# An out projection made of seven block products per half of its inner dimension, with one pooling projection moved ahead

## The chip, the cores and the metric

The kernel runs on one core of a Trainium2 chip. The metric is the device time of one execution in microseconds (us), lower is better; the time before is the median of three runs. One further execution was taken with the hardware profiler. Engines are named as in the profile: PE is TensorE (matmuls), DVE VectorE, ACT ScalarE, POOL GpSimd, SP SyncE; SP and POOL issue most DMAs here.

## The reference

One layer of a streaming encoder on 512 tokens, all in fp32:

```python
h = rmsnorm(x, norm_mix_pre)                 # 512 x 2048
proj = h @ w_in                              # 2048 x 5120: u_pool (1024), q, f, i, g (1024 each)
y_pool = pool_mixer(u_pool, ...)             # windowed means, 4 groups of 256: (mean - u) @ pool_w + b
y_hgrn = hgrn2_mixer(q, f, i, g, ...)        # gated recurrence, 8 heads of 128
mix = concatenate([y_pool, y_hgrn]) @ w_out  # 512 x 2048 @ 2048 x 2048, the "out projection"
x = x + rmsnorm(mix, norm_mix_post)
h = rmsnorm(x, norm_mlp_pre)
ff = square(relu(h @ w_mlp_in)) @ w_mlp_out  # 2048 x 8192 and back
x = x + rmsnorm(ff, norm_mlp_post)
```

## The kernel before

**Precision.** Every matmul operand of the large projections is split in two parts, hi (a cast on ACT) and lo (raw minus hi, a subtraction on DVE), and a product is the sum of three matmuls: hi·hi, hi·lo and lo·hi. A weight block of 512 x 512 (1 MB, "room") is loaded raw by SP, and its split takes two casts and two subtractions of 128 x 1024, by halves.

**Order.** The kernel is written out by hand: each engine takes its instructions in the order in which the Python issues them. Two lists help. `clock` holds generators ("tasks": gates, scores, outputs, pooling), of which each takes a step at a tick, and a tick comes after each block of 12 matmuls. `mplan` and `plan` are tables that say what is issued at which slot of the products. The input projection runs in ten groups of 512 columns, `proj_order`; pooling halves are U0 and U1, the recurrence's halves F, Q, V, G with 0 or 1. `outputs(c)` finishes the recurrence's half c and `task()` of `pool_chunk(c)` the pooling's half c; both also store signed copies into DRAM (`stash`, tile `mix_dram`).

**Out projection.** The left half of the output columns (tiles `om`) is computed plainly: 2 groups x 4 weight blocks x 4 row tiles x 12 = 384 matmuls. The right half uses a form of Strassen's scheme with seven products instead of eight (`ORDER`, numbers 1, 2, 5, 3, 6, 7, 4). The work of one product with one weight block is here called a slot: 24 matmuls of 128 x 512. The right half takes 14 slots, (product, inner half q) in pairs. A slot needs a weight operand and an activation operand. The weight operands of products 1, 5, 6 and 4 live in the same room, which is not reloaded but refilled: after the split of product 1's block a POOL DMA adds another block of `w_out` to it in place, and so on. Products 5, 3, 6 and 7 take activation sums made from `mix_dram` (tiles `sr`), split by `split_sum`. The split for slot m+1 is issued at the start of slot m. Results go from the PSUM banks `oa` and `og` to Y by ACT copies or DVE adds (`evac_half`), and are then squared (ACT) and weighed (DVE).

The MLP that follows uses the same seven products for all of its work and makes up the time from 668 us on.

Of the kernel before, what the change touches and what calls it, by code (L numbers as in the profile page):

```python
# [28 lines left out]
def hybrid_block(  # L29
# [334 lines left out]
    proj_order = (U0, F0, Q0, V0, G0, F1, Q1, V1, G1, U1)  # L364
# [3 lines left out]
    mix_rows = (2, 0, 3, 1)  # L368
    for n in range(2):
        for r in mix_rows:  # L370
            wlist.append((w_out, r, n))
# [82 lines left out]
    mixp = {}  # L454

    def stash(c, q, k, src, scales):

        sg = junk_tile([P, 512], "signed").rearrange("p (t s) -> p t s", t=2)
        for t in range(2):
            nc.scalar.activation(out=sg[:, t], in_=src[:, t * 256:(t + 1) * 256], func=AF.Copy,  # L460
                                 scale=scales[(t + 1 + c) % 2])
        nc.gpsimd.dma_start(mix_dram[c, q].rearrange("t p k s -> p t k s")[:, :, k, :], sg)


    def pool_chunk(c, tags):
# [14 lines left out]
        def task():  # L480
# [21 lines left out]
            dh, dl = new_pair(f"pd{c}")  # L502
# [22 lines left out]
            if c:  # L525
                add(A, B, 4, 7, hi2)
                add(B, A, 8, 15, hi2)
                yield 1
            diff(1, *ws[1])
            split(1, hi2, ws[1][1])  # L530
            yield 1
            ph, pl = new_pair(f"mp{c}")
            mixp[("p", c)] = (ph, pl)
            for g, (w, s) in enumerate(ws):
                for o in range(2):
                    ps = pss.tile([P, 512], F32, tag="s", name="pps")
                    for ct in range(2):
                        wh, wl = (pw[:, k, g, ct, o * P:(o + 1) * P] for k in range(2))
                        j = 2 * g + ct
                        nc.tensor.matmul(ps, wh, dh[:, j], start=ct == 0, stop=False)  # L540
                        nc.tensor.matmul(ps, wh, dl[:, j], start=False, stop=False)
                        nc.tensor.matmul(ps, wl, dh[:, j], start=False, stop=ct == 1)
                    j = 2 * g + o
                    y = U[:, j, PAD:]
                    nc.vector.tensor_scalar(out=y, in0=ps, scalar1=vcol("pb", 4 * c + j),
                                            scalar2=vcol("pscale", 4 * c + j), op0=ALU.add, op1=ALU.mult)
                    nc.scalar.copy(out=ph[:, j, :], in_=y)
                    nc.vector.tensor_tensor(out=pl[:, j, :], in0=y, in1=ph[:, j, :].bitcast(F32), op=ALU.subtract)
                    stash(c, 1, j, y, (1.0, -1.0))
                    yield 1  # L550
# [4 lines left out]
    class Hgrn:  # L555
# [156 lines left out]
        def outputs(self):  # L712
# [20 lines left out]
            ph, pl = new_pair(f"mh{c}")  # L733
            mixp[("h", c)] = (ph, pl)
# [5 lines left out]
            for h in range(4):  # L740
                ps = pss.tile([P, 512], F32, tag="s", name="ops")
                for w in range(NT):
# [3 lines left out]
                nc.scalar.activation(out=ph[:, h, :], in_=ps, func=AF.Copy, scale=g)  # L746
                nc.vector.scalar_tensor_tensor(out=pl[:, h, :], in0=ps, scalar=g, in1=ph[:, h, :].bitcast(F32),
                                               op0=ALU.mult, op1=ALU.subtract)
# [17 lines left out]
    clock.add(lower_bound_task(), 14)  # L766
    for ci, c in enumerate(proj_order):
        gemm_group(f"pj{c}", xT, c not in (V0, V1, G0, G1), evacs[c],
                   feeder=feed_x if ci == 0 else None)
        if c == U0:  # L770
            clock.add(pt0(), 1)
        elif c == U1:
            clock.add(pt1(), 1)
        elif c in (F0, F1):
            clock.add(hgr[c == F1].gates(), 1)
        elif c in (G0, G1):
            clock.add(hgr[c == G1].outputs(), 1)


    class MixActs:  # L780
        order = (("h", 0), ("p", 0), ("h", 1), ("p", 1))

        def __len__(self):
            return 4

        def __getitem__(self, i):
            return mixp[self.order[i]]

    ss_m = const.tile([P, NT, 4], F32, name="ss_m")
    X, YZ, HI, LO, A = {}, {}, {}, {}, {}  # L790

    def late_pools():
# [30 lines left out]
    ss2 = const.tile([P, NT], F32, name="ss2")  # L823
# [37 lines left out]
    def keep_x2(t):  # L861
        Y = late["Y"]
        n_out = (D, D, D // 2, 0)[t]
        if n_out < D:
            nc.sync.dma_start(x2_dram[t * P:(t + 1) * P, 0:D - n_out], Y[t][:, 0:D - n_out])
        if n_out:
            nc.sync.dma_start(out2d[t * P:(t + 1) * P, D - n_out:D], Y[t][:, D - n_out:D])

    def norm2_task():
        for t in range(NT):  # L870
            yv = late["Y"][t]
            nc.scalar.activation(out=yv, in_=yv, func=AF.Square, accum_out=ss2[:, t:t + 1])
# [7 lines left out]

    def evac_mix(n):
        def f(t, bank):
            if n == 0 and t == 0:
                late_pools()
            yv = late["Y"][t][:, n * 512:(n + 1) * 512]
            junk = junk_tile([P, 512], "junk")
            nc.scalar.activation(out=junk, in_=bank, func=AF.Square, accum_out=ss_m[:, t, n:n + 1])
            nc.vector.tensor_tensor(out=yv, in0=bank, in1=late["wpost"][n // 2][:, n % 2 * 512:n % 2 * 512 + 512],
                                    op=ALU.mult)
        return f  # L890

# [100 lines left out]
    def feed_in(tp, u, engine):  # L992

        dst = raw_in(tp, 1 + u // 2, u % 2)
        for k2 in range(2):
            ps = pss.tile([P, 2, 256], F32, tag="s", name="fps")
            for k in range(2):
                c = u * 512 + (2 * k2 + k) * P
                for t in range(2):
                    nc.tensor.transpose(out=ps[:, k, t * P:(t + 1) * P],  # L1000
                                        in_=late["Y"][2 * tp - 2 + t][:, c:c + P], identity=ident)
# [9 lines left out]
    S, SR = {}, {}  # L1011

    def new_sum(i):
        S[i] = pairs.tile([P, 2, 8, 256], F32R, tag="pp", name=f"s{i}")

    def split_sum(i, q):
        src = SR[i][:, 4 * q:4 * q + 4]
        a = S[i][:, :, 4 * q:4 * q + 4]
        if i == 7:
# [7 lines left out]
    def split_sum_step(i, q):  # L1027
        return lambda: split_sum(i, q)

    def load_sums():  # L1030
        yield 1
        for nm, (i0, i1) in (("53", (5, 3)), ("67", (6, 7))):
            room = pairs.tile([P, 2, 8, 256], F32, tag="pp", name=f"sr{nm}")
            SR[i0], SR[i1] = room[:, 0], room[:, 1]
        for q in range(2):
            qs = slice(4 * q, 4 * q + 4)
            for i, (c, tp) in ((7, (0, 1)), (5, (1, 1)), (6, (0, 0)), (3, (1, 0))):
                nc.sync.dma_start(SR[i][:, qs], mix_dram[c, q, tp])
            yield 1

    def sums_task(q):

        a5, a7, a6, a3 = (SR[i][:, 4 * q:4 * q + 4] for i in (5, 7, 6, 3))
        for dst, src in ((a5, a7), (a7, a6), (a6, a5), (a3, a6)):
            nc.vector.tensor_tensor(out=dst, in0=dst, in1=src, op=ALU.add)
            yield 1

    mslots = [(i, q) for i in ORDER for q in range(2)]

    def mix_block(a, b, q):  # L1050
        return w_out[mix_rows[2 * a - 2 + q], 1 + b]

    def mix_split_gen(m):
        if m >= len(mslots):
            yield from split_gen(m - len(mslots))
# [12 lines left out]
        if more:  # L1068
            load_mix(raw, *more, q, True)
        elif i == 2:  # L1070
            load_mix(raw, 2, 2, q)
        elif i == 4:
            load_x(q)
        elif q == 0:
            load_yz(0)

    MY = {}

    def load_mix(raw, a, b, q, add=False):
        src = mix_block(a, b, q)  # L1080
# [22 lines left out]
    for n in range(2):  # L1103
        if n == 1:
            clock.add(load_sums(), 2)
            MY[0] = YZ[0]
            MY[1] = [late["tp2"].tile([P, 2, 512], F32, tag="tmp", bufs=4, name=f"my{h}") for h in range(2)]
            clock.add(sums_task(0), 9)
# [613 lines left out]
```

## Time and profile before

| what | value |
|---|---|
| median of three runs | 1925.89 us (1925.26 to 1927.15) |
| the profiled execution | 1927.38 us, its span 1925.7 us |
| input projection and recurrence | 0 to 497 us of the span |
| out projection, left half (`om`) | 497 to 590 us |
| out projection, right half (14 slots) | 590 to 668 us |
| MLP | 668 to 1926 us |

The profiled execution lies 0.08% above the median. Its span runs from the first to the last instruction; the 1.7 us beside it are start and end. Rows of the timeline give start, duration, engine, line and operation; a bracket at a row's end is the idle time before it and what ended it.

### The profile page before, as it was taken

What the parts mean: (1) busy time and instruction counts of PE and PEld (TensorE: products, weight loads), DVE (VectorE), ACT (ScalarE), POOL (GpSimd) and SP (SyncE); (2) the same over time, 40 slices, a digit from 0 to 9 for tenths busy, and PEclk for the clock granted to TensorE, in tenths of its full rate; (3) what the DMA queues carried; (4) which work ended last, traced back from release to release, by engine and by line L of the source; (5) the groups of instructions that cost most, each with busy time, mean ns of one, the idle gap of its engine ahead of it and who ended that gap; (6) DMA issues with size and microseconds to landing.
All of it is one profiled execution on the core that took longest, in us unless ns stands there. A gap on an engine that the chain in (4) does not pass through costs nothing.

```text
span 1925.7 us, 26162 instructions
## 1 busy us (share of the span) xinstructions
PE 1910.2 (99%) x10864; PEld 1627.3 (85%) x10864; DVE 1277.8 (66%) x1332; ACT 865.2 (45%) x1028; POOL 178.6 (9%) x283
## 2 busy tenths in 40 slices
PE   9999999999999999999999999999999999999997
PEld 7888888888888899888888888888888888888886
DVE  5646343734646777676666665777777878878787
ACT  6421242133325676444454444456544444444455
POOL 3000000000000001111101111011010010010111
PEclk9999999999999999999999999999999999999999
DMA  8322222222367979988988889889898897897987
GB/s 317 110 95 82 88 99 99 89 88 88 110 236 176 295 211 236 224 216 214 216 232 198 219 212 220 264 218 234 215 241 224 195 243 225 205 234 211 232 213 148
DMA packets 60086, 369.25 MB, mean 192 GB/s; under 512 B 6592, under 2 KB 7616, under 8 KB 22208
## 3 DMA queue, kind: packets, MB, share of 16 engines
q0 software_dynamic: 26912, 168.31, 42.2%
q1 hardware_dynamic: 32912, 199.02, 28.6%
q8 instruction: 85, 1.39, 0.3%
q14 instruction: 33, 0.27, 0.0%
q10 hardware_dynamic: 144, 0.26, 0.0%
HBM read 338.20 MB, written 29.36 MB: 191 GB/s over the span
## 4 chain that ended last, share of the span: by engine, by line
PE 97%; DMA 1%; DVE 1%; ACT 1%; issue 0%; SPq 0%; DVEq 0%; ACTq 0%
PE pj L269 23%; PE ps L1304 18%; PE al L1524 16%; PE ga L1524 12%; PE ps L1307 10%; PE om L269 5%; PE la L1524 2%; PE oa L1129 2%; PE og L1319 2%; PE lg L1524 2%; PE og L1129 2%; PE oa L1319 1%; PE lps L645 1%; PE pm L1319 1%; DMA YZ<-in_w_mlp_in 1%; PE po L719 0%
## 5 line engine op out<-in xcount | busy, mean ns | idle before, releaser
L1304 PE MATMUL ps<-a,mh 128*128 128x512 f32 x1536 | 370.6, 391 | 0.0
L1304 PEld LDWEIGHTS ps<-a,mh 128*128 128x128 f32 x1536 | 280.9, 188 | 53.7 <-issue 0.3
L1524 PE MATMUL al<-mh,o 128*128 128x512 f32 x896 | 277.1, 389 | 0.0
L937 ACT CAST mh<-X 128x1024 fp32r<-128x1024 f32 x176 | 180.5, 1055 | 204.3 <-PE ps L1304 82.9
L937 ACT CAST mh<-YX 128x1024 fp32r<-128x1024 f32 x176 | 180.6, 1055 | 158.8 <-PE al L1524 46.3
L938 DVE TENSOR_TENSOR ml<-X,mh 128x1024 fp32r<-128x1024 f32 x176 | 207.4, 1220 | 53.5 <-ACT mh L937 53.3
L269 PE MATMUL pj<-xT,wh 128*128 128x512 f32 x760 | 235.6, 391 | 0.0
L938 DVE TENSOR_TENSOR ml<-YX,mh 128x1024 fp32r<-128x1024 f32 x176 | 207.4, 1220 | 31.0 <-ACT mh L937 30.9
L1524 PE MATMUL ga<-mh,o 128*128 128x512 f32 x672 | 208.0, 389 | 0.0
L229 DVE TENSOR_TENSOR wl<-wr,wh 128x1024 fp32r<-128x1024 f32 (+1 forms) x100 | 117.2, 1181 | 136.0 <-ACT wh L228 136.0
L1307 PEld LDWEIGHTS ps<-a,ml 128*128 128x128 f32 x1536 | 199.6, 191 | 9.0
L1307 PE MATMUL ps<-a,ml 128*128 128x256 f32 x1536 | 202.4, 283 | 0.0
L1524 PEld LDWEIGHTS al<-mh,o 128*128 128x128 f32 x896 | 168.2, 188 | 34.8
L228 ACT CAST wh<-wr 128x1024 fp32r<-128x1024 f32 (+1 forms) x100 | 98.9, 1012 | 193.5 <-PE pj L269 152.8
L1524 PE MATMUL al<-ml,o 128*128 128x512 f32 x448 | 174.3, 389 | 0.0
L269 PEld LDWEIGHTS pj<-xT,wh 128*128 128x128 f32 x760 | 141.5, 188 | 28.8
L269 PE MATMUL pj<-wh,xT 128*128 128x512 f32 x512 | 164.8, 395 | 0.0
L937 ACT CAST mh<-YZ 128x1024 fp32r<-128x1024 f32 x96 | 98.5, 1053 | 129.7 <-PE ps L1304 51.1
L1524 PEld LDWEIGHTS ga<-mh,o 128*128 128x128 f32 x672 | 126.2, 188 | 26.1
L269 PE MATMUL pj<-xT,wl 128*128 128x512 f32 x380 | 148.1, 390 | 0.0
L1353 DVE TENSOR_TENSOR t<-t,ps 128x512 f32<-128x512 f32 x120 | 82.4, 687 | 89.0 <-ACT t L1356 67.8
L938 DVE TENSOR_TENSOR ml<-YZ,mh 128x1024 fp32r<-128x1024 f32 x96 | 113.2, 1221 | 34.7 <-ACT mh L937 34.7
(305 smaller groups left out, 2725.3 us busy)
## 6 DMA issues: line engine op xcount, KB each, us to landing
wr<-in_w_in SPq DMA_DIRECT2D x38, 1024.0 KB, 4.9
X<-in_w_mlp_in POOLq DMA_DIRECT2D x33, 1024.0 KB, 9.4
X<-in_w_mlp_out POOLq DMA_DIRECT2D x33, 1024.0 KB, 8.6
YX<-in_w_mlp_in POOLq DMA_DIRECT2D x23, 1024.0 KB, 9.5
YX<-in_w_mlp_out POOLq DMA_DIRECT2D x23, 1024.0 KB, 8.9
YX<-in_w_mlp_in SPq DMA_DIRECT2D x21, 1024.0 KB, 5.8
YX<-in_w_mlp_out SPq DMA_DIRECT2D x21, 1024.0 KB, 4.9
YZ<-in_w_mlp_in SPq DMA_DIRECT2D x16, 1024.0 KB, 8.9
```

Of the source, the lines that this page charges most:

```text
L228: nc.scalar.copy(out=hi[:, ks, :], in_=raw[:, ks, :])
L229: nc.vector.tensor_tensor(out=lo[:, ks, :], in0=raw[:, ks, :], in1=hi[:, ks, :].bitcast(F32), op=ALU.subtract)
L269: nc.tensor.matmul(bank, l, r, start=first and kt == 0 and oi == 0, stop=last and kt == 3 and oi == 2)
L645: nc.tensor.matmul(tiles[-1][r:r + mb, h % nh, w], K[:, h, w * P + r:w * P + r + mb], rhs[:, b0:b0 + nb, 1, :], start=True, stop=True)
L937: nc.scalar.copy(out=hi[:, ks, :], in_=raw[:, ks, :])
L938: nc.vector.tensor_tensor(out=lo[:, ks, :], in0=raw[:, ks, :], in1=hi[:, ks, :].bitcast(F32), op=ALU.subtract)
L1129: nc.tensor.matmul(bank[h], l, r[:, kt, :], start=i in (1, 2, 5) and q == 0 and kt == 0 and oi == 0, stop=q == 1 and kt == 3 and oi == 2, ...
L1304: nc.tensor.matmul(o, hi[:, kt, ms], r, start=first and kt == 0, stop=q == 1 and kt == 3 and not first, skip_group_check=True)
L1307: nc.tensor.matmul(o[:, 0], lo[:, kt, ms], r[:, 0], start=False, stop=q == 1 and kt == 3, skip_group_check=True)
L1319: nc.tensor.matmul(o, l[:, kt, ms], r[:, x], start=st and oi == 0 and m % 2 == 0, stop=sp and oi == 2, skip_group_check=True)
L1353: nc.vector.tensor_tensor(out=t, in0=t, in1=half(banks, s_), op=sign)
L1524: nc.tensor.matmul(bank[h] if type(bank) is list else bank[:, h, :], a[:, l, kt, ts], r[:, kt, :], start=i in (1, 2, 5) and kt == 0 and oi ...
```

## The change

The whole out projection is now made of block products. The 2048 columns are taken as two halves (n2 = 0 and 1) and the inner dimension as two halves (e = 0: the first halves of pooling and recurrence, e = 1: the second). A slot is (n2, product, e), and there are 28 slots: for n2 = 0 first all seven products with e = 0, then all seven with e = 1 in the order 2, 1, 5, 3, 6, 7, 4; for n2 = 1 the products in pairs of e, as before. The seven products with e = 0 need nothing of the recurrence's second half, so `outputs(1)` runs at ticks inside slots 0 to 4. For this U1 stands ahead of F1 in `proj_order`. The pooling's operand pair is halved (one group at a time). For n2 = 0 each result tile is written twice, first by e = 0 and then added to by e = 1. Output rows lie by column halves (`YL` in the pool `pairs`, `YR` in `yp`), and a few tiles of the MLP change pools accordingly.

The core of the diff:

```diff
-    proj_order = (U0, F0, Q0, V0, G0, F1, Q1, V1, G1, U1)
+    proj_order = (U0, F0, Q0, V0, G0, U1, F1, Q1, V1, G1)
...
-    mslots = [(i, q) for i in ORDER for q in range(2)]
+    mslots = [(0, i, 0) for i in ORDER] + [(0, i, 1) for i in (2, 1) + ORDER[2:]]
+    mslots += [(1, i, e) for i in ORDER for e in range(2)]
+    n_mix = len(mslots)
...
+    def split_sum(n2, i, e):
+        k = sums_made[0] % 2
+        sums_made[0] += 1
+        S[n2, i, e] = ring[-1][:, k]
+        split_into(S[n2, i, e], SR[e][:, TERM[i]], i == 7)
...
     def mix_split_gen(m):
...
-        i, q = mslots[m]
-        raw, hi, lo = X[q] if i in (1, 5, 6, 4) else MY[q], HI[m % 2], LO[m % 2]
+        n2, i, e = mslots[m]
+        raw, hi, lo = (MXW if i in (1, 5, 6, 4) else MY)[n2, e], HI[m % 2], LO[m % 2]
...
         more = {1: (1, 2), 5: (2, 2), 6: (2, 1), 3: (1, 2)}.get(i)
         if more:
-            load_mix(raw, *more, q, True)
+            load_mix(raw, n2, *more, e, True)
...
-    for n in range(2):
...
-        gemm_group(f"om{n}", MixActs(), False, evac_mix(n))
-    clock.drain()
...
+    def second_rooms():
+        late_pools()
+        load_terms(1, 6, 7)
+        MXW[0, 1] = YZ[0]
+        load_mix(YZ[0], 0, 1, 1, 1)
+
+    def second_terms():
+        mixed_room("12b")
+        split_plain(2)
+        split_plain(1)
+        load_wpost(0)
...
     mplan = {
+        3: ([sum_step(0, 6, 0)], []),
+        4: ([sum_step(0, 7, 0)], []),
+        5: ([second_rooms, lambda: split_plain(4), lambda: add_from_dram(5, 0, 1), lambda: add_from_dram(7, 0, 0)], []),
+        6: ([second_terms], []),
+        7: ([add_step(6, 5)], []),
+        8: ([sum_step(0, 5, 1), add_step(3, 6)], []),
+        9: ([sum_step(0, 3, 1), lambda: load_wpost(1)], []),
...
+        24: ([sum_step(1, 7, 1), yx_room, lambda: residual(0, (0, 1))], []),
...
-    for m in range(len(mslots)):
+    for m in range(n_mix):
...
+            clock.tick()
```

Three places show how the instructions stand. In the names, `X`, `YZ`, `MY` and `my` are rooms with raw weights, `mh` and `ml` their hi and lo parts, `sr` and `terms` raw activation sums, `s` and `ring` their split form, `oa` and `og` PSUM banks, `signed` a stashed copy.

The refills on POOL, before, from the first of `w_out` on:

```order
L1084 DMA X0_4364<-in_w_out 128x2048
L1084 DMA X1_4433<-in_w_out 128x2048
L1084 DMA X0_4364<-in_w_out 128x2048
L1084 DMA X1_4433<-in_w_out 128x2048
L1084 DMA YZ0_4144<-in_w_out 128x2048
```

and after, from the last stash of the recurrence on (slots 4 to 12):

```order
L467 DMA mix_dram_85<-signed_4120 128x2x256
L1202 DMA terms1_3869<-mix_dram_85 128x1024 x2
L1079 DMA YZ0_4138<-in_w_out 128x2048 x2
L1079 DMA X1_3829<-in_w_out 128x2048
L1079 DMA YZ0_4138<-in_w_out 128x2048
```

Two rooms take turns before; after, the room YZ0 is refilled twice in a row, for slots 9 and 11, and slots 8 and 9 both read it.

DVE before, over slots 2 to 4 of the right half:

```order
L1025 TENSOR_TENSOR s5_4541<-sr53_4255,s5_4541 128x1024
L1063 TENSOR_TENSOR ml0_4411<-X0_4364,mh0_4410 128x1024 x2
L1025 TENSOR_TENSOR s5_4541<-sr53_4255,s5_4541 128x1024
L1146 TENSOR_TENSOR Y0_4142<-Y0_4142,og0_4473 128x512
L1146 TENSOR_TENSOR Y0_4142<-Y0_4142,og1_4474 128x512
L1153 TENSOR_TENSOR Y0_4142<-Y0_4142,wpost1_4146 128x512 x2
L1063 TENSOR_TENSOR ml1_4470<-X1_4433,mh1_4469 128x1024 x2
```

and DVE after, from the split for slot 9 (issued in slot 8) to the first evacuation of slot 9:

```order
L1053 TENSOR_TENSOR ml1_3858<-YZ0_4138,mh1_3857 128x1024 x2
L1009 TENSOR_TENSOR ring1_4137<-terms1_3869,ring1_4137 128x1024
L1000 TENSOR_TENSOR terms1_3869<-terms1_3869 128x1024
L1151 TENSOR_TENSOR YL_3868<-YL_3868,oa0_3859 128x512
L1151 TENSOR_TENSOR YL_3868<-YL_3868,oa1_3860 128x512
L1160 TENSOR_TENSOR YL_3868<-YL_3868,wpost0_4139 128x512 x2
L1053 TENSOR_TENSOR ml0_3808<-X1_3829,mh0_3807 128x1024 x2
L1009 TENSOR_TENSOR ring1_4137<-terms1_3869,ring1_4137 128x1024
L1151 TENSOR_TENSOR YL_3868<-YL_3868,og0_3861 128x512
```

The operand `ring1` of slot 9 stands behind the split for slot 9, where `s5` was split two slots ahead of its use; the evacuations of slot 8 (`oa0`, `oa1`) and two weighings stand behind both and ahead of everything that slot 10 needs.

SP after, from slot 5 on:

```order
L1081 DMA X0_3760<-in_w_out 128x2048
L992 DMA terms1_3869<-mix_dram_85 128x1024 x2
L1081 DMA YZ0_4138<-in_w_out 128x2048
L1081 DMA X1_3829<-in_w_out 128x2048
L796 DMA wpost0_4139<-in_norm_mix_post 128x1024
```

where before it had, at the start of the right half:

```order
L1086 DMA X0_4364<-in_w_out 128x2048
L1086 DMA X1_4433<-in_w_out 128x2048
L1086 DMA YZ0_4144<-in_w_out 128x2048
L1086 DMA my0_4205<-in_w_out 128x1024
L1086 DMA my1_4206<-in_w_out 128x1024
```

The load of YZ0, which slot 8 reads, now stands behind a load that waits for the split of slot 6 and two loads that wait for the last stash.

More of the change, by code (lines that the diff above doesn't have):

```diff
@@ L531, in task @@
             yield 1
[L532 to L550, printed above, removed]
+            yield from maps(1)
         return evac, task
@@ L764, in chain @@
             yield from g()
[L766 to L787, printed above, removed]
+    first = {}
     ss_m = const.tile([P, NT, 4], F32, name="ss_m")
     X, YZ, HI, LO, A = {}, {}, {}, {}, {}
+    late["Y"], ring = [], []
     def late_pools():
@@ L879, in norm2_task @@
         late["rbc2"] = True
[L881 to L890, printed above, removed]
     NP = DFF // 1024
@@ L1025, in split_sum, with split_plain @@
             nc.vector.tensor_tensor(out=a[:, 1], in0=src, in1=a[:, 0].bitcast(F32), op=ALU.subtract)
[L1027 to L1038, printed above, removed]
+    def split_plain(i):
+        split_into(mixed(i, 1), SR[1][:, TERM[{1: 6, 2: 3, 4: 5}[i]]], i != 2)
@@ L1101, in hybrid_block @@
     behind["split"] = [first_mix_split]
[L1103 to L1108, printed above, removed]
-            clock.add(sums_task(1), 11)
-        gemm_group(f"om{n}", MixActs(), False, evac_mix(n))
-    clock.drain()
+    clock.add(lower_bound_task(), 14)
+    for ci, c in enumerate(proj_order):
+        if c == G1:
+            clock.add(first["sums"](), 5)
+        gemm_group(f"pj{c}", xT, c not in (V0, V1, G0, G1), evacs[c],
+                   feeder=feed_x if ci == 0 else None)
+        if c == U0:
+            clock.add(pt0(), 1)
+        elif c == U1:
+            clock.add(pt1(), 1)
+        elif c in (F0, F1):
+            clock.add(hgr[c == F1].gates(), 1)
+        elif c in (G0, G1):
+            clock.add(hgr[c == G1].outputs(), 1)
     HI[1] = wspl.tile([P, 4, 512], F32R, tag="hi", name="mh1")
@@ new lines, in evac_half @@
+        t, n = 2 * tp - 2 + h, 2 * n2 + b - 1
+        yv = yrow(t, n * 512, (n + 1) * 512)
+        second = n2 == 0 and e == 1
+        src = bank
+        if i in (1, 5, 3, 4) and not second:
+            if i != 4 or n2 == 0:
+                nc.scalar.copy(out=yv, in_=bank)
+                return
+        else:
+            nc.vector.tensor_tensor(out=yv, in0=yv, in1=bank, op=ALU.subtract if i in (6, 7) else ALU.add)
+            src = yv
+        if (n2, e) == (0, 0) or (second and i not in (1, 6, 7, 4)):
@@ L1143, in evac_half @@
             return
-        src = bank
-        if i != 4:
-            nc.vector.tensor_tensor(out=yv, in0=yv, in1=bank, op=ALU.add if i == 2 else ALU.subtract)
-            src = yv
         junk = junk_tile([P, 512], "junk")
         nc.scalar.activation(out=junk, in_=src, func=AF.Square, accum_out=ss_m[:, t, n:n + 1])
-        wp = late["wpost"][1][:, (n - 2) * 512:(n - 1) * 512]
+        wp = late["wpost"][n2][:, (b - 1) * 512:b * 512]
         def weigh():
             nc.vector.tensor_tensor(out=yv, in0=src, in1=wp, op=ALU.mult)
-        if i == 4:
+        if n2 and i == 4:
@@ new lines, in second_rooms, with add_from_dram, third_rooms @@
+    def second_rooms():
[3 more added lines that the diff above has]
+        load_mix(YZ[0], 0, 1, 1, 1)
+    def add_from_dram(i, q, tp):
+        nc.gpsimd.dma_start(SR[1][:, TERM[i]], mix_dram[1, q, tp], accum_op=ALU.add)
+    def second_terms():
[3 more added lines that the diff above has]
+        load_wpost(0)
+    def third_rooms():
+        MY[1, 1] = [late["tp2"].tile([P, 2, 512], F32, tag="tmp", bufs=4, name=f"my{h}") for h in range(2)]
+        load_mix(MY[1, 1], 1, 2, 1, 1)
```

249 lines of the change are left out of this document (152 added, 97 removed).

## The prediction

> **What bounds the kernel now.** I read the page first (busy shares and the chain that ended last), then who waited for whom on PE, then the stages.
>
> ```profile
> span 1925.7 us, 26162 instructions
> PE 1910.2 (99%) x10864; PEld 1627.3 (85%) x10864; DVE 1277.8 (66%) x1332; ACT 865.2 (45%) x1028; POOL 178.6 (9%) x283
> PE 97%; DMA 1%; DVE 1%; ACT 1%; issue 0%; SPq 0%; DVEq 0%; ACTq 0%
> PE fps L1000 <- ACT RU L1005: 1.4, 1, 1.4
> ```
>
> PE is busy for 99% of the span and carries 97% of the chain; its longest wait after the start is 1.4 us. So matmuls taken away are time gained, and a wait put into PE's row is time lost, one for one. The two stages of the out projection (busy us and counts of PE, PEld, DVE, ACT, POOL, then clock, DMA share, GB/s):
>
> ```profile
> 497.00:543.00 46.00, 46.00 (x204) 37.95 (x203) 29.68 (x31) 17.08 (x27) 4.01 (x6) 1.00 0.34 124
> 543.00:590.00 47.00, 47.00 (x209) 38.94 (x208) 23.74 (x24) 11.22 (x18) 0.89 (x1) 1.00 0.62 227
> 629.00:668.00 39.00, 39.00 (x183) 32.42 (x181) 30.33 (x40) 25.04 (x40) 2.54 (x3) 1.00 0.98 301
> ```
>
> The plain half leaves DVE, ACT and the DMA engines room; the product half has DVE at 78% and the DMA engines full. The change makes all of it product work.
>
> **The gain.** 384 plain matmuls go and 14 slots of 24 come: 48 fewer. The busy mean of 0.39 us overlaps the next matmul, so the price is the spacing of the starts:
>
> ```profile
> 620.70 0.39 PE L1129 MATMUL og<-ml,s 128*128 128x512 f32 x1
> 620.93 0.62 PE L1129 MATMUL og<-mh,s 128*128 128x512 f32 x2
> 621.38 0.39 PE L1129 MATMUL og<-ml,s 128*128 128x512 f32 x1
> ```
>
> Three per 0.68 us is 0.227 each: 48 x 0.227 = 10.9 us gained, and a slot lasts 24 x 0.227 = 5.44 us.
>
> **Moved at no cost.** U1's task now runs during F1, whose evacuation needs the same buffer. Before, it ran during `om`:
>
> ```profile
> 531.76 0.72 ACT L460 ACTIVATE signed<-pu 128x256 f32<-128x256 f32 x2
> 538.52 0.60 ACT L887 ACTIVATE junk<-om 128x512 f32<-128x512 f32 x1 [6.04 <-issue]
> ```
>
> Its last stash ended at 532.5, and a group's first evacuation came at 538.5: 6 us of cover; without it F1 would slip by the difference. `outputs(1)` takes the same matmuls in slots 0 to 4 as it did in U1. The added refills of `w_out` (8 MB more on POOL) are hidden wherever a room has two slots or more to refill, save in the rivals.
>
> **The refill chain (slots 8 and 9).** Products 1 and 5 of e = 1 are neighbours and share YZ0. Slot 9's split must wait for a refill which must wait for slot 8's split. The links, from the product half of before:
>
> ```profile
> 613.25 1.98 ACT L1062 CAST mh<-X 128x1024 fp32r<-128x1024 f32 x2
> 614.31 2.36 DVE L1063 TENSOR_TENSOR ml<-X,mh 128x1024 fp32r<-128x1024 f32 x2 [0.25 <-ACT mh L1062]
> 616.59 1.22 DVE L1025 TENSOR_TENSOR s<-sr,s 128x1024 fp32r<-128x1024 f32 x1
> 606.12 2.58 DVE L1063 TENSOR_TENSOR ml<-X,mh 128x1024 fp32r<-128x1024 f32 x2
> 609.00 0.84 POOL L1084 DMA_DIRECT2D X<-in_w_out  x1 [13.70 <-DVE ml L1063]
> X<-in_w_out POOLq DMA_DIRECT2D x6, 1024.0 KB, 8.3
> wr<-in_w_in SPq DMA_DIRECT2D x38, 1024.0 KB, 4.9
> my<-in_w_out POOLq DMA_DIRECT2D x2, 512.0 KB, 13.7
> ```
>
> Let slot 8's split start at s. It ends 3.42 later (613.25 to 616.67); POOL issues 0.30 after that (608.70 to 609.00); the refill lands 8.3 later. Then slot 9's casts, its two subtractions and, behind them on DVE, the operand's subtraction end 4.56 later (613.25 to 617.81). Slot 9's third matmul needs that operand, 0.45 after the first. Slot 9 starts at s + 3.42 + 0.30 + 8.3 + 4.56 - 0.45 = s + 16.1. Slot 8 starts at s + 2.3 (first cast and subtraction), so slot 9 would have started at s + 7.7: it stalls 8.4 us. The floor: if s is slot 7's own start (earlier the hi and lo buffers aren't free), slot 9 is due 10.9 later and stalls 5.2. The ceiling takes the refill at 13.7: 13.8. I take 8.4, for the median of the same DMA.
>
> When is s? YZ0 is loaded in slot 5, on SP behind X0, which waits for slot 6's split (stash 1.3, first cast 1.1, two subtractions 2.36: 4.8 us into slot 5), and behind two terms: 3 MB with it. Before, 3 MB went out in one bunch too:
>
> ```profile
> X<-in_w_out SPq DMA_DIRECT2D x1, 1024.0 KB, 4.8
> YZ<-in_w_out SPq DMA_DIRECT2D x1, 1024.0 KB, 6.8
> my<-in_w_out SPq DMA_DIRECT2D x2, 512.0 KB, 8.7
> ```
>
> So YZ0 lands some 9.5 us after X0's issue, 10.5 with a term's accumulation beside it: s is 15.4 into slot 5. Slot 7 starts at 12.0, slot 8 is due at 17.5 and starts at 17.7: a stall of 0.2 us, between 0 and 3.
>
> **What stands behind it on DVE and ACT (slot 10).** From the end of the operand's subtraction, in the order of the rows: add 1.1, two evacuations 1.3, the rest of the second square 1.0, a cast 1.1, slot 10's subtractions 2.4, its operand 1.1, evacuation of slot 9's first half 0.65. Slot 10 adds to that bank, so it starts 8.65 later, where slot 9 ends at 5.0: 3.7 us, between 0 (if slot 8's rows slip in during the wait, which the order excludes) and 4. Prices:
>
> ```profile
> 609.76 0.68 DVE L1146 TENSOR_TENSOR Y<-Y,og 128x512 f32<-128x512 f32 x1
> 612.44 0.69 DVE L1153 TENSOR_TENSOR Y<-Y,wpost 128x512 f32<-128x512 f32 x1
> 612.62 0.63 ACT L1149 ACTIVATE junk<-Y 128x512 f32<-128x512 f32 x1 [1.42 <-DVE Y L1146]
> 613.16 0.19 ACT L1149 ACTIVATION_READ_ACCUMULATOR junk<-Y 128x1 f32 x1
> ```
>
> The idle PE may come back slow: the kernel's first matmuls lasted 648 ns, and eight of them 3.78 us, 0.47 each.
>
> ```profile
> L256 PE MATMUL pj<-xT,wh 128*128 128x512 f32 x8 | 3.8, 648 | 0.6 <-ACT wh L228 0.6
> ```
>
> Up to 15 such matmuls in slot 9 (15 x 0.245 = 3.7) are covered by slot 10's wait, so I cost them at 0; all 24 would add 2.2.
>
> **Slots that are merely full.** In slots 11 to 13 DVE has a split 2.3, an operand 1.1, two evacuations 1.25 and two weighings 1.25, up to 5.9 against 5.44, with the evacuation that the next slot needs last: 2.2 over three slots, between 0 and 4. In slot 4 the four normalisations hold the operand back 0.65, and in slot 6 the stash ahead of the casts holds the evacuation back 1.15: 1.8, between 0 and 2.5.
>
> ```profile
> 467.93 2.50 DVE L737 TENSOR_TENSOR G<-G,rh 128x512 f32<-128x512 f32 x4
> 472.98 0.48 ACT L460 ACTIVATE signed<-ops,vec 128x256 f32<-128x256 f32 x1 [0.82 <-DVE mh L747]
> 647.81 2.35 DVE L1063 TENSOR_TENSOR ml<-my,mh 128x1024 fp32r<-128x1024 f32 x2
> ```
>
> Slot 24 does what slot 10 of before did, where the split ended at 650.16, 6.06 after that slot's start (590 + 10 x 5.44); now an operand's 1.14 follows, needed at 5.89: 1.3, between 0 and 2.
>
> **Sum.** -10.9 + 1.8 + 0.2 + 8.4 + 3.7 + 2.2 + 1.3 = +6.7 us. Against the profiled 1927.4 that is 1934.1. The median of the runs shown is 1.5 lower, so the forecast for it is 1925.9 + 6.7 = 1932.6 us: slower by 0.35%. A measurement of this kernel can tell about 0.2% (3.9 us) from no change.
>
> **Rivals.**
>
> 1. *DVE and ACT keep up* (not slower). The order puts the late rows behind one another, but engines that run 66% and 45% busy may do them inside the waits. Then 1.8, 3.7, 2.2 and 1.3 go and only the refill is paid: -10.9 + 8.6 = -2.3, 1923.6 us, no change. It speaks against it that `oa` and `og` are added to from slot to slot, so the evacuation must come first. If besides YZ0 lands within slot 6, the stall is at its floor and the sum -10.9 + 5.2 = -5.7, 1920.2 us. It decides for "faster" where all stalls together stay below 7.0 us.
>
> 2. *The refill meets other transfers.* In the last product slots of before (DMA share 0.98) a refill landed in 13.7 us. With the terms and weighings loaded just ahead of it, slot 9's may take that too: +5.4, 1938 us.
>
> 3. *The refill is quick.* If it lands like a plain load, in 4.9 us: -3.4, 1929.2 us, no change. [...]
>
> 4. *TensorE's work doesn't shrink*: the code has 28 x 24 = 672 matmuls for 720, so this is out.
>
> **How the numbers follow.** Forecast 0.50 (its own range 1930 to 1937), rival 2 0.14, rival 1 without its floor 0.18 and with it 0.11, rival 3 0.07. Slower: 0.64; same: 0.18 + 0.07 = 0.25; faster: 0.11. The range 1920 to 1941 takes in rival 1's floor and rival 2 with a second late refill, and leaves out some 0.1 in all.
>
> **What would show it.** 672 matmuls of `oa` and `og` with 128 x 512 operands and none of `om`; slots of 5.44 us. PE idle of about 8 us ahead of the tenth slot, in which ACT waits for the DMA into YZ0, and 3 to 4 us ahead of the next, put down to DVE. The POOL refill of `w_out` about 8 us. No PE waits between 240 and 500 us. The prediction is wrong if ACT's wait for that refill is short, or if PE's other waits come to less than 2 us.

## The result, and the profile after

The changed kernel takes 1949.94 us (median of four runs, 1948.79 to 1952.39) against 1926.04 us of the kernel before in the same session (1925.26 to 1927.15): ratio 1.0125, interval 1.0108 to 1.0143, so slower by 24 us. The forecast was 1932.6, with 1941 as its upper end. The profiled execution took 1949.39 us, its span is 22.0 us longer than before's. First the page of the changed kernel:

```profile
span 1947.7 us, 26198 instructions
PE 1910.2 (98%) x10816; PEld 1621.6 (83%) x10816; DVE 1309.0 (67%) x1370; ACT 887.3 (46%) x1063; POOL 186.8 (10%) x291
```

48 matmuls fewer, as forecast, and yet PE is "busy" for the same 1910.2 us: some of the remaining matmuls must have become longer. DVE gained 31 us of work. Next, who let PE wait (total, times, longest; us), where before had 3.8 us in four waits:

```profile
PE og L1132 <- ACT ring L1008: 7.4, 1, 7.4
PE oa L1132 <- DVE YL L1151: 5.3, 3, 3.6
PE pps L522 <- ACT mx L514: 4.2, 2, 2.7
...
PE pps L523 <- DVE mx L515: 1.2, 2, 0.8
PE og L1132 <- DVE YL L1151: 1.0, 1, 1.0
```

The first row is the forecast stall at slot 9. The third and fourth were in no term of the prediction: `pps` are the pooling's maps, far ahead of the out projection. Where the 22 us lie is read from matmuls that both programs have. The rows give start and duration; the first row of each kernel is the first matmul of group V0, the second the first transpose, which stands ahead of the last slot's products, the third the first matmul `ps` of the MLP. Before:

```profile
145.56 0.39 PE L269 MATMUL pj<-wh,xT 128*128 128x512 f32 x1
...
660.60 0.60 PE L1000 MATMUL fps<-ident,Y 128*128 128x128 f32 x4
...
769.55 0.40 PE L1304 MATMUL ps<-a,mh 128*128 128x512 f32 x1
```

After:

```profile
152.27 0.39 PE L269 MATMUL pj<-wh,xT 128*128 128x512 f32 x1
...
679.51 0.38 PE L976 MATMUL fps<-ident,YL 128*128 128x128 f32 x2
...
791.33 0.40 PE L1351 MATMUL ps<-a,mh 128*128 128x512 f32 x1
```

The changed kernel is late by 6.7 us at the first place, 18.9 at the second, 21.8 at the third, and keeps that to the end. So 6.7 us went before the out projection was reached, 12.2 in it (a gain of 10.9 and losses of 23.1), and 2.9 in the MLP's first slots. The windows of the changed kernel show what the waits alone don't (us; then PE, PEld, DVE, ACT, POOL busy with counts, granted clock, DMA share, GB/s):

```profile
60.00:71.00 11.00, 7.80 (x21) 5.56 (x20) 6.74 (x10) 3.31 (x6) 0.69 (x1) 0.69 0.28 95
544.00:553.00 9.00, 6.59 (x18) 5.21 (x19) 7.01 (x8) 4.39 (x6) 0.92 (x1) 0.62 0.81 251
573.00:580.00 7.00, 6.35 (x15) 4.54 (x16) 6.50 (x8) 3.57 (x8) 0.84 (x1) 0.55 0.68 119
```

In each of these stretches, just behind a wait, the granted clock is 0.55 to 0.69, and the matmuls start 0.43 us apart instead of 0.227. That is the missing length. Summing over the rows of PE how much later each matmul starts than 0.227 us after the one ahead of it gives, by places:

| place | waits | slow matmuls and rounding | lost | forecast |
|---|---|---|---|---|
| pooling's maps, 60.8 to 82 us | 5.45 | 3.85 | 9.3 | 0 |
| slot 4 | 0.17 | 0.17 | 0.3 | 0.65 |
| slot 6 | 3.57 | 2.85 | 6.4 | 1.15 |
| slot 9 | 7.85 | 3.1 | 11.0 | 8.4 |
| slot 10 | 1.04 | 0.16 | 1.2 | 3.7 |
| slots 12 to 14 (forecast for 11 to 13) | 1.73 | 0.3 | 2.0 | 2.2 |
| slot 25 | 1.02 | 0.16 | 1.2 | 1.3 |

The places in the out projection sum to 22.1 us, 1.0 short of the 23.1 that the common matmuls give; the rest is spread in pieces too small to list. The pooling's 9.3 us became 6.7 at the first common matmul because this execution started 2.7 us quicker: its first eight matmuls took 2.14 us where the profiled execution of before needed 3.78. All ten profiled executions of the changed kernel and of its variants below were quicker here, by 1.7 to 2.7 us at the 240th matmul of the projection; with a single trace of before, no run shows whether the change or chance is behind that.

```profile
6.00 2.14 PE L256 MATMUL pj<-xT,wh 128*128 128x512 f32 x8
```

### The profile page after: what moved, and what is told of

Read it like the earlier page. It is cut to its first block, busy times and chain, and to the rows that moved or that the text cites. A ratio compares the mean times of both kernels' runs of the same rounds, so it can differ in the third digit from the quotient of the medians.

```text
span 1947.7 us, 26198 instructions
## 1 busy us (share of the span) xinstructions
PE 1910.2 (98%) x10816; PEld 1621.6 (83%) x10816; DVE 1309.0 (67%) x1370; ACT 887.3 (46%) x1063; POOL 186.8 (10%) x291
## 4 chain that ended last, share of the span: by engine, by line
PE 65%; DVE 2%; DMA 1%; ACT 1%; issue 1%; DVEq 0%; ACTq 0%
PE ps L1351 18%; PE al L1571 16%; PE ga L1571 12%; PE ps L1354 9%; PE oa L1132 2%; PE la L1571 2%; PE og L1366 2%; PE lg L1571 2%; PE og L1132 2%; DMA YZ<-in_w_mlp_in 1%; DVE ml L914 1%; PE oa L1366 1%; DVE ml L1053 1%; DMA X<-in_w_out 0%; DMA YZ<-in_w_out 0%
## 5 line engine op out<-in xcount | busy, mean ns | idle before, releaser
L228 ACT CAST wh<-wr 128x1024 fp32r<-128x1024 f32 (+1 forms) x84 | 82.5, 1007 | 180.3 <-PE pj L269 142.0
L229 DVE TENSOR_TENSOR wl<-wr,wh 128x1024 fp32r<-128x1024 f32 (+1 forms) x84 | 97.7, 1172 | 94.8 <-ACT wh L228 94.8
L914 DVE TENSOR_TENSOR ml<-YZ,mh 128x1024 fp32r<-128x1024 f32 x96 | 113.1, 1220 | 34.4 <-ACT mh L913 34.4
```

The costliest lines, as they stand in the source:

```text
L228: nc.scalar.copy(out=hi[:, ks, :], in_=raw[:, ks, :])
L229: nc.vector.tensor_tensor(out=lo[:, ks, :], in0=raw[:, ks, :], in1=hi[:, ks, :].bitcast(F32), op=ALU.subtract)
L914: nc.vector.tensor_tensor(out=lo[:, ks, :], in0=raw[:, ks, :], in1=hi[:, ks, :].bitcast(F32), op=ALU.subtract)
```

## The experiments

The stage time in the following is the time from the first matmul of slot 0 to the first transpose of the last slot: 178.3 us in the changed kernel (501.24 to 679.51). Ratios are against the kernel before, in the same session; the changed kernel's is 1.0125.

**The pooling's maps.** Both groups of a pooling half now share one operand pair. So the first group's matmuls stand right behind the first split and the second split stands behind them. The maps come after 240 matmuls of the projection, one tick (12 matmuls, 2.7 us) earlier than before, where it was 252. This run puts them after 264.

```diff
             add(B, A, 2, 3, hi2)
-            yield 1
+            yield 1 if c else 3
...
             split(1, hi2, ws[1][1])
-            yield 1
+            yield 1 if c else 2
             yield from maps(1)
```

> The pooling's first maps come two ticks (24 matmuls, 5.4 us) later, its second ones a tick later; nothing else is changed. In the changed kernel PE waited 2.74, 0.46, 1.49 and 0.76 us for the split of the shared operand pair (5.45 us) and ran slow for another 3.9: by spacing the matmuls between 60.8 and 82 us lost 9.4. Theory A (each stall is a cost of its own, wait and slow clock together): the waits at the pooling's matmuls vanish and the time falls by 9.4 to about 1940.5 us. Rival B (the start of the kernel made up for part of it: a common landmark at 160 us lies only 6.7 us later than before): 1943. Rival C (U1's move, not the shared pair, costs the time): no change, 1950.

1942.15 us, ratio 1.0079 (1.0064 to 1.0094): 8.9 us less by the ratios. In the changed kernel the split ended at 65.18, 4.1 us after the maps' turn had come (61.07, one spacing behind the last matmul in front of them):

```profile
63.95 1.23 DVE L515 TENSOR_TENSOR mx<-pa,mx 128x1024 fp32r<-128x1024 f32 x1 [1.17 <-ACT mx L514]
63.97 0.80 PE L522 MATMUL pps<-mx,ps 128*128 128x512 f32 x1 [2.74 <-ACT mx L514]
```

With two ticks more the maps find it done, and slot 0 starts at 492.60 instead of 501.24, 8.6 us earlier:

```profile
67.20 0.39 PE L522 MATMUL pps<-mx,ps 128*128 128x512 f32 x1
```

The waits and the slow matmuls at the maps are gone, and the first matmul of slot 0 gained what they had cost, as theory A says. The time alone doesn't tell A from B: it lies between their 1940.5 and 1943, and the intervals of the two ratios are wider than that. C is out: U1's move costs nothing, as the absence of any wait of PE between 83 and 501 us says too.

**Slot 6: the store on another queue.** In the changed kernel ACT stood still ahead of slot 6's casts:

```profile
539.63 0.48 ACT L465 ACTIVATE signed<-ops,neg_hnw 128x256 f32<-128x256 f32 x1 [4.88 <-DMA mix_dram<-signed]
541.08 2.01 ACT L1052 CAST mh<-X 128x1024 fp32r<-128x1024 f32 x2
```

and the evacuation that PE waited for stood behind this on DVE. First try:

```diff
-        nc.gpsimd.dma_start(mix_dram[c, q]...[:, :, k, :], sg)
+        queue = nc.sync if (c, q) == (1, 0) else nc.gpsimd
+        queue.dma_start(mix_dram[c, q]...[:, :, k, :], sg)
```

> The recurrence's second half stores its signed copies by SP instead of POOL. Theory A: in slot 5 ACT waited 4.88 us for the store of an earlier copy, which POOL had issued 2 us late behind a refill and which then shared the DMA engines with it; the casts for slot 6 stood behind that wait, PE waited 3.57 us and ran slow for 2.6 us more. With the store on SP, ACT's wait falls below 1.5 us, slot 6 starts on time and the time falls by about 6 us to 1944. YZ0, which is loaded after the last store, comes earlier by as much as slot 9, whose stall stays at 7 to 8 us. Rival B (DMA engines, not the queue, are what the store waits for): ACT's wait stays above 3 us, the time within 2 us of 1950. Rival C (SP in order: loads of weights stand behind stores): a new wait of PE for a cast in slots 2 to 6, 1950 or more.

1951.34 us, ratio 1.0126 (1.0111 to 1.0141): no gain. The wait moved to the next copy and grew:

```profile
542.87 0.47 ACT L465 ACTIVATE signed<-ops,neg_hnw 128x256 f32<-128x256 f32 x1 [6.04 <-PE oa L1133]
```

PE is named, but it had long made what this copy reads; what was missing was a room, since an earlier copy's store was still under way, as the next run shows. Rival B holds: the queue isn't the reason, a store issued on SP just behind that refill took 10.0 us. In the changed kernel the two stores behind a refill took as long as the refill (8.6 us, of the stores the median), a later one with no refill beside it 2.5 (out<-in, queue, count, size, us to landing; three windows):

```profile
X<-in_w_out POOLq DMA_DIRECT2D x1, 1024.0 KB, 8.6
mix_dram<-signed POOLq DMA_DIRECT2D x2, 256.0 KB, 8.6
...
mix_dram<-signed POOLq DMA_DIRECT2D x1, 256.0 KB, 2.5
```

**Slot 6: a room for each copy.**

```diff
+        if (c, q) == (1, 0):
+            if k == 0:
+                copies.append(hgp.tile([P, 4, 512], F32, tag="Q", name="copies"))
+            sg = copies[0][:, k].rearrange("p (t s) -> p t s", t=2)
+        else:
             sg = junk_tile([P, 512], "signed").rearrange("p (t s) -> p t s", t=2)
```

> The four signed copies of the recurrence's second half get a room of their own each (the recurrence's dead operand Q) instead of two shared ones; they are stored by POOL as in the changed kernel. With the store on SP, ACT had waited 6.0 us for a store all the same, so the store's duration and the two rooms are now the suspects. Theory A (two rooms): ACT's wait of 4.9 us goes, the split for slot 6 starts at about 536 us instead of 541, PE's 3.57 us of wait and 2.7 us of slow matmuls go: -6.3, about 1944 us from the changed kernel's 1949.9. Rival B (given back): YZ0's load stands on SP behind terms that wait for the same stores, so it lands no earlier; slots 8 and 9 then wait as much longer as slot 6 starts earlier, and the time stays at 1948 to 1950.

1946.71 us, ratio 1.0105 (1.0091 to 1.0118): 3.9 us less by the ratios, whose intervals overlap, so the time alone doesn't show a gain. The stage time is 177.3 (499.84 to 677.15), only 1.0 less; another 1.4 us lie ahead of slot 0, where this execution lost 7.6 us at the pooling's maps instead of 9.3. ACT's wait for a store is gone and PE's at slot 6 fell from 3.57 to 1.77. A longer wait at slot 10 (the first row below) and a new one at slot 8 (the last) took the place, and slot 9 still waited 6.4 us:

```profile
PE og L1139 <- DVE YL L1158: 2.1, 1, 2.1
PE oa L1139 <- DVE YL L1158: 1.8, 1, 1.8
...
PE oa L1139 <- ACT mh L1059: 1.6, 1, 1.6
```

Slot 8 waited for the casts of YZ0, the first of which began at 554.85, when the load had landed. So within the stage the gain is given back, as rival B forecast, but not for its reason. The terms didn't wait for the stores: the last store had landed by 540.4, and SP issued the terms at 541.80, 0.5 us behind X0's load, which had waited for slot 6's split. That split came only 1.9 us earlier than in the changed kernel, counted from slot 0, and YZ0 landed 12.0 us after its issue (11.8 in the changed kernel).

**The refill between slots 8 and 9.** The chain in the changed kernel, by rows of POOL, ACT and DVE:

```profile
558.99 2.36 DVE L1053 TENSOR_TENSOR ml<-YZ,mh 128x1024 fp32r<-128x1024 f32 x2 [5.50 <-ACT mh L1052]
561.88 0.84 POOL L1079 DMA_DIRECT2D YZ<-in_w_out  x1 [5.75 <-DVE ml L1053]
570.24 1.99 ACT L1052 CAST mh<-YZ 128x1024 fp32r<-128x1024 f32 x2 [10.34 <-DMA YZ<-in_w_out]
573.60 1.22 DVE L1009 TENSOR_TENSOR ring<-terms,ring 128x1024 fp32r<-128x1024 f32 x1
582.44 1.28 DVE L1151 TENSOR_TENSOR YL<-YL,og 128x512 f32<-128x512 f32 x2
```

Split, issue 0.5 us later, landing 8.3 later, split, operand: the links of the prediction. To take the refill away, the second block is loaded into a free room and DVE adds:

```diff
+        if (n2, i, e) == (0, 1, 1):
+            for h in range(2):
+                ks = slice(2 * h, 2 * h + 2)
+                nc.vector.tensor_tensor(out=X[0][:, ks], in0=X[0][:, ks], in1=YZ[0][:, ks], op=ALU.add)
...
-        MXW[0, 1] = YZ[0]
+        MXW[0, 1] = X[0]
         load_mix(YZ[0], 0, 1, 1, 1)
+        load_mix(X[0], 0, 1, 2, 1)
```

> In the e = 1 half, product 1's block stays in YZ0 and product 5's second block is loaded plainly into X0, which is free; DVE adds the two (2.4 us), so that no refill stands between slots 8 and 9. X0 goes on with products 6 and 4, and the two rooms change places for n2 = 1. Theory A (the refill is the cause of slot 9's stall): the wait of 7.4 us and the slow 3.4 us behind it go; X0 lands behind YZ0, so up to 2 us of wait may stay; slot 10's wait (1.0) and part of slot 12's (1.6) go too: 1949.9 - 10.8 - 1 + 1 = about 1939 us (1937 to 1942). Rival B (DVE in order is the real limit of slots 8 to 13, the added 2.4 us make it worse): the waits return in slots 9 to 13 as waits for DVE, 1945 or more.

1940.44 us, ratio 1.0075 (1.0060 to 1.0090): 9.6 us less by the ratios, the stage time 170.3, 8.0 less. The 7.4 us are gone; what waits at slot 9 is the operand behind DVE's added sum (1.8), and slot 10 still waits:

```profile
PE og L1142 <- DVE ring L1009: 1.8, 1, 1.8
...
PE og L1142 <- DVE YL L1161: 1.5, 1, 1.5
```

Theory A for the refill; a part of B for what stands behind it.

**Is it idleness that makes PE slow?** Matmuls without use were put into the waits:

```diff
+            def fill(n):
+                warm = pss.tile([P, 512], F32, tag="s", name="warm")
+                for k in range(n if c == 0 else 0):
+                    nc.tensor.matmul(warm, pw[:, 0, 0, 0, 0:P], pw[:, 0, 0]..., start=True, stop=True)
...
                 mixed_room("12a")
+                fill(14)
             yield from maps(0)
```

> Matmuls whose result is not used are put into PE's waits: 14 ahead of the pooling's first maps, 6 ahead of its second, 28 ahead of slot 9. Theory A (PE is slow after a wait because it was idle): the matmuls behind these waits are spaced by 0.227 us instead of 0.43. At the pooling 3 to 4 us are won. In slot 9 3.4 us are won, but slot 10 stands behind a chain of DVE that doesn't depend on PE (it ran without a gap from 571.3 to 583.7 us), so its wait grows from 1.0 to about 4.4. Sum: about 1946.5 us. Rival B (slot 10 follows PE): 1943. Rival C (the slow matmuls have another cause, such as traffic of DMA and DVE at that moment): spacing stays 0.43, the filling costs what doesn't fit, 1950 to 1953.

1957.77 us, ratio 1.0161 (1.0144 to 1.0178). The matmuls ahead of slot 9 read the hi tile into which slot 10's split writes, so they waited 14.2 us for that split; the total therefore says nothing of that place. At the pooling the answer is clear. Behind the filling the maps start 0.23 us apart (0.43 in the changed kernel):

```profile
61.68 3.38 PE L560 MATMUL warm<-ps 128*128 128x512 f32 x14
64.90 0.40 PE L522 MATMUL pps<-mx,ps 128*128 128x512 f32 x1
65.14 0.39 PE L523 MATMUL pps<-mx,ps 128*128 128x512 f32 x1
```

and slot 0 starts 2.4 us earlier (498.79), though 20 matmuls (4.5 us) were added ahead of it. For slot 9 it was done again, with operands that are ready:

```diff
+        if m == 9:
+            warm = pss.tile([P, 512], F32, tag="s", name="warm")
+            for k in range(32):
+                nc.tensor.matmul(warm, MX["12b"][:, 0, 0, 0:P], MX["12b"][:, 0, 0:2]..., start=True, stop=True)
         products_mix(m, mhook)
```

> 32 matmuls without use (7.3 us) ahead of slot 9 alone, with operands that are ready by then; in the earlier filling run those ahead of slot 9 read the weights of slot 10 and so waited 14.2 us by themselves, which told nothing of this place. Theory A (idle time makes PE slow; slot 10 hangs on a chain of DVE): slot 9's matmuls stand 0.227 us apart, 3.4 us are won there, and the wait ahead of slot 10 grows from 1.0 to about 4.4: the time stays at 1950. Rival B (slot 10 follows PE): 1946.5. Rival C (traffic makes slot 9 slow): spacing stays 0.43, 1950.

1949.81 us, ratio 1.0118 (1.0103 to 1.0134). Theory A: slot 9 ran at 0.227 us, and the wait ahead of slot 10 grew from 1.0 to 3.1 us, since DVE's chain ends when it ends; after that wait slot 10 was slow instead:

```profile
564.80 7.41 PE L1277 MATMUL warm<-mx12b 128*128 128x512 f32 x32
584.05 0.47 PE L1132 MATMUL og<-mh,ring 128*128 128x512 f32 x1 [3.09 <-DVE YL L1151]
585.54 0.63 PE L1132 MATMUL og<-ml,ring 128*128 128x512 f32 x1
```

**All of it mended.** The pooling's ticks, the rooms for the copies, the sum by DVE (with YZ0's load ahead of the terms), and slot 24's reciprocal root behind its split:

```diff
-            rstd_of(0)
...
-        24: ([sum_step(1, 7, 1), yx_room, lambda: residual(0, (0, 1))], []),
+        24: ([sum_step(1, 7, 1), lambda: rstd_of(0), yx_room, lambda: residual(0, (0, 1))], []),
```

> All mended at once: the pooling's maps two ticks and one tick later; a room for each of the four copies; product 5's weights by a plain load into X0 and DVE's sum, with YZ0's load ahead of the terms on SP; the four-row reciprocal root of slot 24 behind its split. Theory A (the stalls are separate): before's 1926.9 - 10.9 for 48 matmuls, + 0.3 (slot 4), + 3 (slots 10 and 12, where DVE was full in the run with the added sum too), + 1.5 (the MLP's first slots): about 1921, 1918 to 1923. Rival B (DVE is what limits slots 7 to 13, where it ran without a gap for 20 us): the removed waits come back there, 1925 to 1930.

1930.01 us, ratio 1.0020 (1.0011 to 1.0029): 20 us better than the changed kernel and still slower than before. The expectation of theory A was too low by 9; the upper end of rival B came out. The stage time is 166.5, and from the last slot's first transpose to `ps` it took 113.1 us (before: 109.0, the changed kernel: 111.8), in part because the matmuls behind the MLP's short waits ran slow here (2.3 us of waits, 1.3 of slow matmuls).

```profile
PE og L1149 <- DVE YL L1168: 3.1, 1, 3.1
...
PE oa L1383 <- DVE ml L921: 1.7, 5, 0.8
...
PE og L1149 <- DVE ring L1016: 1.6, 1, 1.6
```

**The order of DVE's work.** On top of that kernel:

```diff
-        5: ([second_rooms, lambda: split_plain(4), ...], []),
+        5: ([second_rooms], [lambda: split_plain(4), ...]),
-        7: ([add_step(6, 5)], []),
-        8: ([sum_step(0, 5, 1), add_step(3, 6)], []),
+        7: ([add_step(6, 5), sum_step(0, 5, 1), sum_rooms], []),
+        8: ([add_step(3, 6)], []),
...
+            if m == 9:
+                evac_half(8, h)
...
-        if m < n_mix - 2:
+        if 14 <= m < 22 and weighs:
+            weighs.pop(0)()
+        if m < 8 or 22 <= m < n_mix - 2:
             run_weighs()
```

Here `sum_rooms` is DVE's sum of the two weight rooms, which stood in slot 8's split. In the second norm's task, a `yield 1` now also stands ahead of the mean.

> As the mended kernel (1930.0), with DVE's and ACT's work put in the order of need: weighings of the first column half wait until slots 14 to 21; the operand of slot 9 and the first sum of terms are made in slot 7, ahead of DVE's sum of the two weight rooms; slot 8's results are taken out after slot 9's first halves; the plain split for slot 13 stands behind slot 5's first evacuation; the second norm's mean comes one tick later. The mended kernel's trace lost 1.93 us at slot 6, 2.09 at slot 9, 4.7 at slot 10 (3.1 of it a wait, 1.4 slow matmuls), 0.6 at slots 12 and 13, 4.2 in the MLP's first slots (2.3 waits, 1.3 slow). Theory A (order, not DVE's amount of work, makes these waits): 0.7 remain at slot 6, about 1 at slots 9 and 10, 1 to 2 in the MLP: 1930 - 1.2 - 5.8 - 2.5 = about 1920.5, 1918 to 1923, faster than before. Rival B (DVE is full from slot 7 to slot 13 whatever the order): the wait at slot 10 moves to slots 11 to 14, 1927 to 1930.

1926.27 us, ratio 0.9998 (0.9989 to 1.0007): level with before, not faster. The MLP's first slots took 109.1 us, 4.0 less than in the mended kernel and as in the kernel before: that loss was the second norm's mean, which had stood on DVE ahead of the work for the next slot. The stage fell only from 166.5 to 165.4, where 7 us were expected. The longest wait of PE there is 1.4 us; waits of 0.7 to 1.4 us stand at slots 6, 9, 10, 11 and 12:

```profile
PE oa L1144 <- DVE YL L1163: 2.4, 2, 1.4
...
PE og L1144 <- DVE ml L1061: 1.2, 1, 1.2
```

**What limits that.**

```diff
             if add and n2 == 0 and e == 1:
+                nc.gpsimd.dma_start(dst, src[:, ks])
+            elif add:
                 nc.gpsimd.dma_start(dst, src[:, ks], accum_op=ALU.add)
```

> The reordered kernel with the refills of slots 9 to 12 (n2 = 0, e = 1; products 5, 6 and 3) issued by POOL as plain loads: the old block is overwritten instead of added to, so the sums of weight blocks are left out. Nothing else changes. The reordered kernel (1926.3) lost 1.9 us at slot 11 and 1.6 at slot 12, where ACT waited 0.9 and 3.1 us for refills of X that landed about 8.6 us after their issue. Theory A (the adding makes the refill long, and a room that is refilled every second slot has no slack: 3.4 for the split, 8.6 for the refill against 10.9): a plain load by POOL lands in about 5 us, the waits of slots 11 and 12 fall below 0.5 us, the time falls by 3 to about 1923. Rival B (POOL's queue, not the adding, makes it long): landing stays above 8 us, no change. Rival C (DVE's order alone makes those waits): landing at 5 us, but the time stays at 1925.5 to 1926.5.

1922.56 us, ratio 0.9981 (0.9971 to 0.9990): 3.3 us less by the ratios; the stage time fell by 2.6 to 162.7. The three plain loads landed after these times (us at the end of each row, three windows), where the reordered kernel's refills needed 8.3, 10.9 and 7.9. There the second was issued 3.4 us behind the first, and slot 12's cast waited for it:

```profile
X<-in_w_out POOLq DMA_DIRECT2D x1, 1024.0 KB, 7.3
...
X<-in_w_out POOLq DMA_DIRECT2D x1, 1024.0 KB, 6.3
...
X<-in_w_out POOLq DMA_DIRECT2D x1, 1024.0 KB, 5.0
```

The first two overlap each other here too. Theory A in kind: with products one after another for the same e, a room is refilled every second slot (10.9 us), while a split (3.4) and a refill (8.3, the first one's value) take 11.7 together. Slot 12's loss fell from 1.7 to 0.3 us, slot 11's only from 2.1 to 1.1, where less than 0.5 was expected. Some 5 us of loss in the stage stay with DVE's order and the operands; which of them, no run here settles.

## Why the prediction failed, step by step

- *The gain* (10.9 us for 48 matmuls) was right.
- *The refill chain* was right in mechanism: 8.4 us were forecast for slot 9, 7.85 us of waits were measured (7.44 for the operand's cast, 0.41 for its subtraction, both behind the refill into YZ0). Run e3 shows the cause. The refill took 8.3 us, the term's value.
- *Slot 10* was forecast at 3.7 us and lost 1.2. The prediction had said that slow matmuls in slot 9 would be covered by slot 10's wait. They were: 3.1 slow and 1.2 of loss make 4.3, and slots 9 and 10 together lost 12.2 us where 12.1 were forecast. The chain itself was sized well: slot 10 began 8.45 us after the operand's subtraction, forecast 8.65. The filled run turned the one into the other.
- *Slots 4 and 25* came within 0.4 us of their terms. The working of the latter has a slip: 650.16 lies 5.76 us behind 590 + 10 x 5.44, not 6.06, so the term is 1.0 instead of 1.3; 1.2 were lost.
- *Slots 11 to 13* lost 2.0 us where 2.2 were forecast, and that was luck. Its figures don't give the sum (5.9 against 5.44, three times, is 1.4), and DVE wasn't full there. Slot 12 alone lost 1.8, because its cast waited for a refill of X issued at 581.68 that landed 8.9 us later; DVE stood idle for 2.0 us ahead of the subtraction:

```profile
590.65 2.00 ACT L1052 CAST mh<-X 128x1024 fp32r<-128x1024 f32 x2 [5.74 <-DMA X<-in_w_out]
591.74 2.36 DVE L1053 TENSOR_TENSOR ml<-X,mh 128x1024 fp32r<-128x1024 f32 x2 [2.02 <-ACT mh L1052]
```

  That room is refilled every second slot, and the prediction had taken such refills as hidden "wherever a room has two slots or more". Run e9, where such refills are shorter (6.3 us for slot 12's instead of 10.9), nearly removed slot 12's loss: two slots were too few.
- *Slot 8* lost 0.1 us where 0.2 were forecast, and that was luck too. YZ0 landed 13.3 us after X0's issue (544.56 to 557.8), where 10.5 had been reckoned; slot 6 came so late that this was covered. In the run with rooms for the copies slot 6 lost only 2.0 us, and slot 8 lost 4.5.
- *"Slots that are merely full"*, slot 6: the step named the right instruction (the copy to be stored, ahead of the casts on ACT) and sized only its work, 1.15 us. It lost 6.4. The copy's two rooms were still held by stores that had been issued behind a refill and landed with it (8.6 us, of the stores the median, and 8.6 for the refill); PE then idled 3.57 us and lost 2.85 more to slow matmuls. The prediction had counted each queue's instructions and not what a store holds up when it is late.
- *"Moved at no cost"* is the step that failed by most: 0 forecast, 9.3 lost. It looked at U1, the group that the change moves, and found its cover. The cost arose at U0, which isn't moved: the same edit halves the operand pair of both pooling halves, so that maps and splits alternate. The maps of before had no cover to lose: they started at 66.50, in the very moment in which the split that they need ended, and the changed code asks for them one tick earlier, 2.7 us. With the quick start of that execution PE's turn came another 2.7 us earlier and the split's end only 1.3 (65.18), so that the second map, the first to need the whole split, began 3.9 us late (65.23 instead of 61.30). "The pooling's operand pair is halved" was read as a matter of rooms only. Both rows of before, which the prediction did not look at:

```profile
65.28 1.23 DVE L508 TENSOR_TENSOR pd<-pa,pd 128x1024 fp32r<-128x1024 f32 x1 [1.17 <-ACT pd L507]
66.50 0.39 PE L540 MATMUL pps<-pd,ps 128*128 128x512 f32 x1
```

- *The clock* was priced at 0, with a bound of 2.2 us. It was the general error: 9.8 us of the losses at the pooling, slot 6 and slot 9 are slow matmuls behind waits, and only the 3.1 of slot 9 had a cover.
- *The MLP* had no term. 2.9 us were lost there. In run e8, where the second norm's mean comes a tick later, PE's waits behind that mean are gone; the same change had rearranged it.
- *Rival 1* (DVE and ACT keep up) is out. *Rivals 2 and 3* too: slot 9's refill took 8.3 us, neither 13.7 nor 4.9. The refills up to slot 15 took 7.8 to 9.1 us, later ones up to 11.3.

Of the 17.3 us between forecast and result, 6.7 are the pooling (net of the quick start), 5.3 slot 6, 2.9 the MLP; the rest are small terms and the spread between executions. That the total of the out projection without slot 6 came close to its sum owes something to the two lucky terms.

## What to carry to other kernels

Where an edit halves a buffer or makes two steps share one, go through every user of the buffer, not only the step that the change is about, and ask of each consumer by how much its input was early: "no wait" may mean that the input came in the same moment. In the changed kernel the waits of PE at the pooling, slot 6 and slot 9 (5.45, 3.57 and 7.85 us) cost their length and 3.85, 2.85 and 3.1 us of slow matmuls besides; the 3.1 were covered by the chain ahead of slot 10. A room that is refilled every second slot needs split and refill together to be shorter than two slots (here 3.4 and 8.3 us against 10.9).

## What was not expected of the hardware

The granted clock fell at waits that are quite short, but not at each of them. In the changed kernel it was 0.50 from 63.9 to 70.7 us, from 545.2 to 552.0 and from 569.1 to 579.3, and 1.00 between these stretches and behind the last. The wait of 2.74 us at the pooling ended as the first of them began, and the waits of 3.57 us at slot 6 and 7.44 at slot 9 lie across the beginning of the other two; behind the first wait the matmuls were 0.43 us apart until 70.9. At the later waits of 1.49 and 0.76 us at the pooling, of 1.04 at slot 10 and of 1.55 at slot 12 the clock stayed at 1.00. In the run that filled slot 9 alone a wait of 1.71 us in the MLP, ahead of 16 transposes, was followed by matmuls of 256 columns that started 0.21 us apart until 720.8, and 0.12 us apart behind that. Five stretches of the changed kernel (columns as before; the clock is the first number after the counts); the first holds the wait of 2.74 us, the fourth and fifth the waits of 1.49 and 0.76 us:

```profile
60.50:63.90 3.40, 0.73 (x4) 0.26 (x2) 2.24 (x3) 1.03 (x1) 0.00 (x0) 1.00 0.76 243
63.92:67.30 3.38, 2.87 (x6) 1.98 (x7) 2.39 (x2) 0.00 (x0) 0.00 (x0) 0.50 0.15 63
67.34:70.73 3.39, 3.39 (x9) 2.62 (x9) 1.57 (x3) 2.06 (x5) 0.42 (x1) 0.50 0.00 0
77.57:80.96 3.39, 1.76 (x7) 0.91 (x5) 2.17 (x4) 1.04 (x1) 0.00 (x0) 1.00 0.72 226
80.98:84.38 3.40, 2.80 (x12) 2.33 (x13) 1.42 (x3) 0.49 (x2) 0.00 (x0) 1.00 0.27 113
```

What decides whether the clock falls was not shown.

Two stores of 256 KB that were issued right behind a 1 MB refill took 8.6 us like the refill (the median of the two), one on SP's queue 10.0 us, and a later one without a refill beside it 2.5 us.
